# A mixture-of-experts kernel: the two fp32 x loads and the b1 load all issued by SyncE

## The chip, the core and the metric

The kernel runs on one core of one Trainium2 chip. The core has five engines that run side by side and wait for each other by semaphores: TensorE (PE in the profile, with its weight loads as PEld), VectorE (DVE), ScalarE (ACT), GpSimd (POOL) and SyncE (SP). Sixteen DMA engines move data between memory and the core; SP, ACT and POOL can issue transfers to them, each through a queue of its own (in the profile q1 for SP, q10 for ACT, q0 for POOL). The metric is the device time of one execution in microseconds (us), lower is better. The kernel before took 186.33 us, the median of four runs (185.84 to 186.41).

## The reference

Eight experts, each with its own two-layer network, its own 256 tokens of width 512, and 2048 hidden units. All inputs and the output are fp32.

```python
def reference(x, w1, w2, b1, b2):     # x (8,256,512)  w1 (8,512,2048)  w2 (8,2048,512)
    h = np.matmul(x, w1) + b1[:, np.newaxis, :]          # b1 (8,2048)
    h = np.maximum(h, 0)
    return (np.matmul(h, w2) + b2[:, np.newaxis, :]).astype(np.float32)   # b2 (8,512)
```

One expert's w1 and w2 are 4 MB each in fp32, so the weights are 64 MB in all, and each weight is used for 256 tokens.

## The kernel before, in words

**Two products per expert.** `first_product(e)` computes the hidden layer transposed. For each of 16 blocks of hidden units, four matmuls (L110) accumulate in PSUM a 128x256 block (128 hidden units, 256 tokens), and one ACT instruction (L117) adds b1, applies the ReLU and writes fp16. `second_product(e)` multiplies by w2: a small matmul puts b2 into the accumulator (L151), then 16 matmuls (L163) for each half of the tokens; DVE and ACT copy the two halves out (L130, L131), and a store goes out on SP (L137), for the last expert in four pieces on SP and ACT (L134, L135). The second product runs three experts behind the first (`LAG = 3`).

**Loads of weights.** w1 and w2 are loaded by POOL (L71, L82, and L90 for the last expert's w2 in six pieces), which converts them to fp16 on the way, so that 2 MB arrive for 4 MB read. They all use POOL's one queue. There are three buffers for w1 and three for w2. The list `loads` sets their order: per step x of an expert, w1 of that expert, then w2 of the expert three behind. Everything marked `ordered` keeps its program order on its engine. So the first three w1 loads are issued at once, and the fourth (for expert 3) waits on POOL until the first product of expert 0 has released its buffer.

**Loads of x.** Experts 2 to 7 get x through POOL's queue as fp16 (L65). The first two experts (`nXF32 = 2`) are loaded as fp32 into `x32`, outside of POOL's queue (L176), and DVE casts them (L189). x must stand transposed for the first product: eight TensorE transposes into PSUM (L97) and one DVE copy (L103) per expert.

**The stage in front, where the change is.** b1 is loaded as 16 rows of 1024 (`b1_rows`, L177), transposed by 64 small matmuls against an fp32 identity (L194), and copied by two DVE instructions to `b1T` (L202), the bias of every L117. On TensorE the program order is: the 64 matmuls of b1, the transposes of x of expert 0, the first product of expert 0. On DVE it is: cast of x of expert 0, cast of x of expert 1, the two copies to `b1T`, the copy of the transposed x. On ACT the program order before the first L117 is: load of x of expert 1 (L176), load of b1 (L177). On SP there is one load, x of expert 0, ahead of the first store, which it issues at 72 us.

Of the kernel before, what the change touches and what calls it, by code (L numbers as in the profile page):

```python
# [11 lines left out]
def kernel(  # L12
# [9 lines left out]
    nc = tc.nc  # L22
# [5 lines left out]
    nTB = T // P  # L28
# [25 lines left out]
    b1_rows = singles.tile([E * 2, M // 2], fp32)  # L54
# [14 lines left out]
    def load_w1(e):  # L69
        w1_sb[e] = w1_pool.tile([P, nKC, M], fp16, tag="w1", name="w1sb")  # L70
        ordered(nc.gpsimd.dma_start(  # L71
            out=w1_sb[e], in_=w1[e].rearrange("(p kc) m -> p kc m", kc=nKC)
        ))
# [99 lines left out]

    x32 = singles.tile([P, nXF32, nTB, H], fp32)
    for e in range(nXF32):
        (nc.sync if e == 0 else nc.scalar).dma_start(out=x32[:, e], max_dma_last_dim=2048, in_=x[e].rearrange("(p tb) h -> p tb h", tb=nTB))  # L176
    nc.scalar.dma_start(out=b1_rows, in_=b1.rearrange("e (s i) -> (e s) i", s=2))  # L177
    load_w1(0)
    ordered(nc.gpsimd.dma_start(  # L179
        out=b2_sb,  # L180
        in_=b2.rearrange("e h -> (e h)").rearrange("(o f) -> o f", o=1),
# [10 lines left out]
    for j in range(nJ):  # L192
        for s in range(2):
            ordered(nc.tensor.matmul(  # L194
                out=pb[s * 64 : (s + 1) * 64, j, :, :],
# [5 lines left out]
    for s in range(2):  # L201
        nc.vector.tensor_copy(  # L202
            out=b1T[s * 64 : (s + 1) * 64, :, :], in_=pb[s * 64 : (s + 1) * 64, :, :, s]
# [58 lines left out]
```

## Time and profile before

| | before |
|---|---|
| median of four runs | 186.33 us |
| the profiled execution's own time | 185.84 us |
| its span, first to last instruction | 183.9 us |
| PE busy, and mean granted clock | 139.8 us (76% of the span), 0.916 |
| ACT busy | 62.8 us (34%) |
| DVE busy | 13.4 us (7%) |
| DMA, all queues | 40.57 MB written, 221 GB/s over the span |
| share of the 16 DMA engines: q0 / q1 / q10 | 91.4% / 6.6% / 1.3% |

The profiled execution is the shortest of the four runs. Its span is 1.94 us shorter than its time: launch and end lie outside of it. The shares of the queues say how much of the sixteen DMA engines' time each one's packets took; their sum is close to 100%. Bytes are counted as written, so a weight load counts half of what it reads.

### The profile page before, as it was taken

The page shows a single profiled execution, that of the slowest core. Times are in us where ns is not written, and L with a number is a line of the kernel's source. Part 1 is how long each engine was busy: PE and PEld are TensorE (multiplying, and loading weights), DVE is VectorE, ACT ScalarE, POOL GpSimd, SP SyncE. Part 2 cuts the span into 40 slices and gives each one's busy share as a digit, 9 for nine tenths or more (in the row PEclk, how much of TensorE's full clock was granted, in tenths as well). Part 3 has the DMA queues.
Part 4 walks back from the last instruction along what each step waited for, and adds up shares of the span by engine and source line. Part 5 has one row for each costly group of instructions (what it writes and reads, how often), then busy time and mean ns, then how long its engine had stood idle before and what let it go on. Part 6 is the DMA issues. An engine that isn't in the chain of part 4 may idle for free.

```text
span 183.9 us, 2209 instructions
## 1 busy us (share of the span) xinstructions
PE 139.8 (76%) x946; PEld 99.6 (54%) x946; DVE 13.4 (7%) x22; ACT 62.8 (34%) x138; POOL 16.9 (9%) x37
## 2 busy tenths in 40 slices
PE   0546999399631999429994499946999994999991
PEld 0534889279521747328464374645649741344680
DVE  0320001001000110001100101001010010010101
ACT  0022689458540604505035060352408701010101
POOL 7100030300300002000110000100006100100000
PEclk9999999969995799956999659997899999699999
DMA  5998999899999999899999999999999999999993
GB/s 190 280 221 180 228 228 225 180 222 228 230 217 185 225 228 228 171 278 203 203 228 231 261 200 221 228 233 237 215 228 228 227 227 225 249 230 227 244 221 114
DMA packets 6488, 40.57 MB, mean 221 GB/s; under 512 B 688, under 2 KB 1728, under 8 KB 4432
## 3 DMA queue, kind: packets, MB, share of 16 engines
q0 software_dynamic: 4320, 35.14, 91.4%
q1 hardware_dynamic: 1568, 4.46, 6.6%
q10 hardware_dynamic: 592, 0.85, 1.3%
q8 instruction: 7, 0.11, 0.2%
q14 instruction: 1, 0.01, 0.0%
HBM read 71.39 MB, written 4.19 MB: 411 GB/s over the span
## 4 chain that ended last, share of the span: by engine, by line
DMA 58%; PE 34%; another core or an unknown queue 3%; POOL 2%; issue 1%; ACT 0%; ACTq 0%; POOLq 0%
DMA x<-in_x_dram 25%; DMA w2sb<-in_w_dram 21%; PE acc L163 20%; DMA w1sb<-in_w_dram 12%; PE ph L110 11%; PE psx L97 1%; PE acc L151 1%; POOL w1sb L71 1%; ACT out L131 0%; POOL b_sb L179 0%; POOL w2sb L82 0%; POOL ident masks.py:199 0%; ACTq L135 0%; POOL ident masks.py:197 0%
## 5 line engine op out<-in xcount | busy, mean ns | idle before, releaser
L110 PE MATMUL ph<-xT,w1sb 128*128 128x256 f16 x512 | 69.4, 303 | 8.8 <-DMA w1sb<-in_w_dram 8.8
L117 ACT ACTIVATE hT<-ph,b1T 128x256 f16<-128x256 f32 x128 | 57.0, 473 | 46.4 <-PE ph L110 46.3
L110 PEld LDWEIGHTS <-w1sb 128*128 128x128 f16 x512 | 62.1, 149 | 15.4 <-DMA w1sb<-in_w_dram 9.8
L163 PE MATMUL acc<-w2sb,hT 128*128 128x512 f16 x224 | 51.2, 388 | 2.3 <-DMA w2sb<-in_w_dram 2.3
L163 PEld LDWEIGHTS <-hT 128*128 128x128 f16 x288 | 28.0, 99 | 32.6 <-issue 7.9
L131 ACT COPY out<-acc 128x512 f32<-128x512 f32 (+1 forms) x9 | 4.9, 541 | 60.6 <-PE acc L163 60.6
L97 PE MATMUL psx<-ident,x 128*128 128x128 f16 x64 | 6.6, 265 | 22.7 <-DMA x<-in_x_dram 22.0
L97 PEld LDWEIGHTS <-x 128*128 128x128 f16 x64 | 5.3, 128 | 23.7 <-DMA x<-in_x_dram 22.9
L103 DVE COPY xT<-psx 128x1024 f16<-128x1024 f16 x8 | 5.5, 691 | 84.3 <-PE psx L97 84.3
L130 DVE COPY out<-acc 128x512 f32<-128x512 f32 (+1 forms) x9 | 5.7, 632 | 74.1 <-PE acc L163 74.1
L71 POOL DMA_DIRECT2D w1sb<-in_w_dram x8 | 4.4, 554 | 69.0 <-PE ph L110 68.2
L82 POOL DMA_DIRECT2D w2sb<-in_w_dram x8 | 4.3, 536 | 56.7 <-PE acc L163 56.7
L194 PE MATMUL pb<-ident,b_rows 16*64 16x16 f32 x64 | 3.7, 265 | 6.6 <-DMA b_rows<-in_b_dram 6.6
L163 PE MATMUL acc<-w,hT 128*128 128x256 f16 x64 | 7.4, 273 | 0.1
L194 PEld LDWEIGHTS pb<-ident,b_rows 16*64 16x64 f32 x64 | 3.6, 198 | 6.5 <-issue 6.5
L117 ACT ACT_TABLE_LOAD x1 | 1.3, 1283 | 11.0 <-DVE b1T L202 11.0
L151 PE MATMUL acc<-b_sb,ones 1*128 1x512 f16 (+1 forms) x18 | 4.8, 355 | 0.0
L90 POOL DMA_DIRECT2D w<-in_w_dram x6 | 3.6, 613 | 13.5 <-DMA w2sb<-in_w_dram 13.5
L65 POOL DMA_DIRECT2D x<-in_x_dram x6 | 3.3, 546 | 0.5 <-DMA w1sb<-in_w_dram 0.5
L151 PEld LDWEIGHTS <-ones 1*128 1x128 f16 x18 | 1.1, 92 | 2.1 <-issue 2.1
L189 DVE CAST x<-x 128x1024 f16<-128x1024 f32 x2 | 1.5, 734 | 4.3 <-DMA x<-in_x_dram 4.2
L202 DVE COPY b1T<-pb 64x128 f32<-64x128 f32 x2 | 0.6, 288 | 3.6 <-PE pb L194 3.6
(8 smaller groups left out, 2.0 us busy)
## 6 DMA issues: line engine op xcount, KB each, us to landing
w1sb<-in_w_dram POOLq DMA_DIRECT2D x8, 2048.0 KB, 33.6
w2sb<-in_w_dram POOLq DMA_DIRECT2D x6, 2048.0 KB, 47.6
out_dram<-out SPq DMA_DIRECT2D x7, 512.0 KB, 9.3
w2sb<-in_w_dram POOLq DMA_DIRECT2D x2, 1024.0 KB, 25.3
x<-in_x_dram POOLq DMA_DIRECT2D x6, 256.0 KB, 40.2
w<-in_w_dram POOLq DMA_DIRECT2D x3, 512.0 KB, 32.8
x<-in_x_dram ACTq DMA_DIRECT2D x1, 512.0 KB, 5.3
x<-in_x_dram SPq DMA_DIRECT2D x1, 512.0 KB, 4.4
```

The source lines that it names most:

```text
L71: ordered(nc.gpsimd.dma_start(out=w1_sb[e], in_=w1[e].rearrange("(p kc) m -> p kc m", kc=nKC)))
L82: ordered(nc.gpsimd.dma_start(out=t[:, lo : lo + step, :], in_=src[:, lo : lo + step, :]))
L90: ordered(nc.gpsimd.dma_start(out=t, in_=src[:, lo:hi, c0:c1]))
L97: ordered(nc.tensor.transpose(out=pt[:, kc, tb * P : (tb + 1) * P], in_=x16[e][:, tb, :].rearrange("p (q kc) -> p q kc", kc=nKC)[:, :, kc] ...
L103: nc.vector.tensor_copy(out=xT[e], in_=pt)
L110: ordered(nc.tensor.matmul(out=ph, lhsT=w1_sb[e][:, kc, :].rearrange("p (q j) -> p q j", j=nJ)[:, :, j], rhs=xT[e][:, kc, :], start=(kc == 0),
L117: nc.scalar.activation(out=hT[e][:, j, :], in_=ph, func=mybir.ActivationFunctionType.Relu, bias=b1T[:, j, e : e + 1], scale=1.0,)
L130: nc.vector.tensor_copy(out=out_sb[:, 0, :], in_=po[0])
L131: nc.scalar.copy(out=out_sb[:, 1, :], in_=po[1])
L151: ordered(nc.tensor.matmul(out=t, lhsT=ones1, rhs=b2_sb[0:1, e * H + c0 : e * H + c1], start=True, stop=False,))
L163: ordered(nc.tensor.matmul(out=acc[c0, tb], lhsT=hT[e][:, j, tb * P : (tb + 1) * P], rhs=t[:, j - lo, c0 - p0 : c1 - p0], start=False, sto ...
L194: ordered(nc.tensor.matmul(out=pb[s * 64 : (s + 1) * 64, j, :, :], lhsT=b1_rows.rearrange("r (q j) -> r q j", j=nJ)[:, :, j], rhs=ident[0 ...
```

## The change

The load of x of expert 1 and the load of b1 are issued by SP instead of ACT. All three loads of the front are then one after the other on SP: x of expert 0, x of expert 1, b1. Sizes, pieces and destinations stay as they are, and so do the instructions of TensorE, VectorE and GpSimd and their order. ACT's first instruction becomes the loading of its function table for L117, and ACT's first transfer is the store at L135 at the very end.

```diff
     for e in range(nXF32):
-        (nc.sync if e == 0 else nc.scalar).dma_start(out=x32[:, e], max_dma_last_dim=2048, in_=x[e].rearrange("(p tb) h -> p tb h", tb=nTB))
-    nc.scalar.dma_start(out=b1_rows, in_=b1.rearrange("e (s i) -> (e s) i", s=2))
+        nc.sync.dma_start(out=x32[:, e], max_dma_last_dim=2048, in_=x[e].rearrange("(p tb) h -> p tb h", tb=nTB))
+    nc.sync.dma_start(out=b1_rows, in_=b1.rearrange("e (s i) -> (e s) i", s=2))
     load_w1(0)
```

## The prediction

> **What bounds the kernel now.** I read the page's list of engines first: PE is busy for 76% of the span, no other compute engine for more than 34%. The queues add up to 99.5% of the sixteen DMA engines. So the first question is whether those engines ever rest. Busy time by stretches (columns: stretch in us, its length, PE, PEld, DVE, ACT and POOL busy, granted clock, DMA share, GB/s written):
>
> ```profile
> 1.00:2.00 1.00, 0.00 (x0) 0.00 (x0) 0.00 (x0) 0.00 (x0) 0.76 (x2) 1.00 0.23 20
> 2.00:3.00 1.00, 0.00 (x0) 0.00 (x0) 0.00 (x0) 0.00 (x0) 0.98 (x4) 1.00 0.78 231
> 3.00:4.00 1.00, 0.00 (x0) 0.00 (x0) 0.00 (x0) 0.00 (x0) 1.00 (x4) 1.00 1.00 377
> 4.00:5.00 1.00, 0.00 (x0) 0.00 (x0) 0.00 (x0) 0.00 (x0) 1.00 (x3) 1.00 1.08 416
> ...
> 100.00:140.00 40.00, 32.33 (x191) 21.60 (x192) 2.77 (x4) 12.24 (x28) 1.67 (x4) 0.87 1.04 230
> 140.00:178.00 38.00, 35.65 (x206) 20.29 (x205) 2.07 (x3) 7.81 (x17) 3.46 (x6) 0.96 1.02 235
> 178.00:180.00 2.00, 1.94 (x18) 1.45 (x15) 0.42 (x1) 0.37 (x1) 0.00 (x0) 1.00 0.39 55
> 180.00:184.00 4.00, 0.22 (x3) 0.00 (x0) 0.42 (x1) 0.37 (x1) 0.00 (x0) 1.00 0.40 131
> ```
>
> The second last column is what counts. From 3 us to 178 us the DMA engines are full; only the first microseconds and the last six are not. The bytes are the same after the change. So the end can move in three ways: the DMA engines begin earlier or later, they run dry somewhere because PE releases a weight buffer too late, or the tail changes.
>
> Next the front in order of time (start, duration, engine, line, what, and in brackets the idle time before and what ended it):
>
> ```profile
> 0.73 0.51 ACTq L176 DMA_DIRECT2D x<-in_x_dram  x1
> 0.74 0.42 SPq L176 DMA_DIRECT2D x<-in_x_dram  x1
> ...
> 1.26 0.49 ACTq L177 DMA_DIRECT2D b_rows<-in_b_dram  x1
> ...
> 5.18 1.55 DVE L189 CAST x<-x 128x1024 f16<-128x1024 f32 x2 [4.20 <-DMA x<-in_x_dram]
> ...
> 6.58 3.71 PE L194 MATMUL pb<-ident,b_rows 16*64 16x16 f32 x64 [6.58 <-DMA b_rows<-in_b_dram]
> 10.33 0.59 DVE L202 COPY b1T<-pb 64x128 f32<-64x128 f32 x2 [3.59 <-PE pb L194]
> ...
> 12.05 0.69 DVE L103 COPY xT<-psx 128x1024 f16<-128x1024 f16 x1 [1.13 <-PE psx L97]
> ...
> 15.55 6.66 PE L110 MATMUL ph<-xT,w1sb 128*128 128x256 f16 x36 [3.54 <-DMA w1sb<-in_w_dram]
> ```
>
> The reader is to see two clocks that meet at 15.55. The b1 chain starts when b1 lands (6.58) and ends with the transposed x at 12.05 + 0.69 = 12.74. The first weights land at about 15.5. So the b1 chain has 15.55 - 12.74 = 2.81 us to spare.
>
> Third, the rows of transfers (issues, size of one, median us from issue to landing), and for the first 7 us the packets of each queue:
>
> ```profile
> out_dram<-out SPq DMA_DIRECT2D x7, 512.0 KB, 9.3
> x<-in_x_dram ACTq DMA_DIRECT2D x1, 512.0 KB, 5.3
> x<-in_x_dram SPq DMA_DIRECT2D x1, 512.0 KB, 4.4
> ```
>
> ```profile
> q1 hardware_dynamic: 272, 0.52, 24.1%
> q10 hardware_dynamic: 304, 0.59, 23.0%
> ```
>
> **The change, part by part.** The built program shows that the change does what it says: ACT loses two DMA issues, SP has three in a row, PE's and POOL's order is the same, and DVE's two casts only wait on exchanged semaphores.
>
> *ACT without its two issues.* ACT saves 0.51 + 0.49 us between 0.73 and 1.75. Its next work, the table load, starts at 11.00, held by the `b1T` copy. Worth nothing.
>
> *SP with two more.* At 0.42 us an issue, x of expert 1 is issued at about 1.16 instead of 0.73, and b1 at about 1.58 instead of 1.26. SP's next instruction is a store at 72.13, so nothing is queued behind them. The cost can only come from the packets.
>
> *The packets.* q1 and q10 together bring 0.52 + 0.59 = 1.11 MB, and at the 416 GB/s of the stretch from 4 to 5 us this takes 2.67 us of all lanes, whichever queue they stand in. x of expert 0, alone for a time, lands sooner than its 4.4 us; x of expert 1 and b1 follow in the same queue. If one queue keeps the lanes as full as two, b1 lands when it did, about 6.5. Bounds: the stretch from 2 to 3 us is filled to 0.78, so closing its gap gains at most 0.22 us; if the second load opens a gap as long as its later issue, 0.42 us are lost. q10's stretches without q1 are not told apart in these rows, so I take the middle near zero, +0.1. For the end of the span this is -0.22 to +0.42, because the weights follow on the same lanes and stay full to 178 us.
>
> *b1's chain.* Later by 0.42, or by 0.85 at most (two whole issues), it ends at 13.2 to 13.6 instead of 12.74 and is hidden by the wait for the first weights at 15.55. It is the first cover. If it goes, there is a second: the fourth w1 load is issued only when PE is done with expert 0's first product, at 26.02 on POOL. At that time the third w1 load still occupies the DMA engines, and PE waits for it:
>
> ```profile
> 36.98 5.83 PE L110 MATMUL ph<-xT,w1sb 128*128 128x256 f16 x36 [3.26 <-DMA w1sb<-in_w_dram]
> ```
>
> So the fourth could be issued up to 36.98 - 26.02 = 10.96 us later before the lanes run dry. Only a b1 that lands later by more than 2.81 + 10.96 = 13.8 us, at about 20.3, moves the end. Before that PE is merely late for weights that are not there yet.
>
> *The casts on DVE.* The first may start earlier than 5.18, the second follows x of expert 1; both are done before b1's matmuls end at 10.29. Nothing.
>
> *The tail.* ACT's first transfer of the program is now the store at L135, on the path to the end:
>
> ```profile
> 179.84 0.99 SPq L134 DMA_DIRECT2D out_dram<-out  x2
> 180.00 0.37 ACTq L135 DMA_DIRECT2D out_dram<-out  x1
> ...
> 180.82 0.35 ACTq L135 DMA_DIRECT2D out_dram<-out  x1
> ```
>
> These stores land 2.1 us after issue, the last at 182.9, and the span ends at 183.9. The trace does not show what a first use of ACT's queue costs. The nearest row is the pair of x loads: issued at the same time, with the same size, ACT's landed after 5.3 us and SP's after 4.4. If all of the 0.9 us is first use and the second store queues behind the first, the end is 0.9 later; if only the first store is late it lands at 180.00 + 2.1 + 0.9 = 183.0, 0.1 later; if the 0.9 us is the sharing of lanes, it is 0. Nothing speaks for a gain. I take 0, since the issue at 180.82 has its own landing time and two loads that share 2.67 us of lanes cannot both be first.
>
> *Sum.* -0.22 to +0.42 in front, 0 to +0.9 in the tail: -0.2 to +1.3, likeliest +0.1. Against the profiled execution (span 183.9 and 1.94 around it, 185.84, the shortest of the four) that is 185.9; against the median 186.33 it is 186.4.
>
> **A rule against the row.** The seven output stores of 512 KB take 9.3 us where the load of the same size at the start took 4.4: a small transfer that meets the weight stream takes turns with it. The Trainium skill, "DMA: Bandwidth & Descriptors", section on queues, rings and completion order, says why: each DMA engine goes round the queues that have work, packet by packet. By this rule three loads in one queue get every second turn against the weights, where two queues got two turns of three; this speaks against the change, but only for what is left when the weights begin, and would give a later b1 inside the first cover, so +0. The same page's section on issuing engines says that issuing from several engines saves only issue time; by it the sum would be 0 as well, with 0.85 us as the price on SP. The rows of the front (1.00 and 1.08 full from 3 us on) agree with the second; no row of before shows what the first makes of these loads.
>
> **Rivals.**
> *The tail, slower.* ACT's first transfer is paid at the end instead of in front. For it: the 0.9 us between the x loads, and that the path ends with this store. Against: both loads wanted the same lanes. Price +0.9: 187.2. It decides from +0.56 us (0.3%) on, so from a first use that costs more than about 0.65 in both stores.
> *b1 caught behind the weights, slower.* If the weights reach the lanes before the single queue has been served, x of expert 1 and b1 take turns with large weight packets. A store of 512 KB took 9.3 us in that way, its longest 15.4. q10's count (304 packets for 0.59 MB) says that x comes in pieces of 2 KB, 256 of them; q1's stores have 4 KB rows, 128, so x would need twice as many turns: 18.6 to 30.8 us. Issued at 1.16, it would land at 20 to 32, b1 after it, against the 20.3 from which the lanes run dry: +0 to +12, so 186.4 to 198. For it: q10's load lands at 6.0, close to when the weights start. Against: from 3 to 5 us the lanes are full with 1.11 MB of x and b1, and the same bytes fit again. With a few pieces left behind, the two covers take it.
> *A front that is faster.* Closing the gap from 2 to 3 us gives -0.22: 186.1, inside 0.3%. No row gives more.
>
> **How the numbers follow.** 0.3% of 186.33 is 0.56 us, about what a measurement of this kernel can tell from no change (the four runs themselves spread over 0.57). Covers hold, within 0.3%: 0.58. Tail: 0.17, slower. b1 behind the weights by enough to matter: 0.08, slower. Causes that I can't name, such as the granted clock in PE's last 24 us, which runs at 0.93 to 1.00 without a wait: 0.13 faster, 0.04 slower. So faster 0.13, same 0.58, slower 0.29. The range holds the first case, the small gain and the tail: 185.7 to 187.3, which leaves out the 0.08 and about half of the unnamed.
>
> **What would show it.** Right: the first L110 still at 15.4 to 15.7, behind a wait for w1; b1's first matmul between 6.3 and 7.4; the first cast before 5.18; DMA share 1.0 from 3 to 178 us; the ACT stores landing after 2.0 to 2.2 us. Wrong in front: b1's first matmul after 9.4, then PE's first L110 moves; after 20, then the DMA share drops near 37 us. Wrong in the tail: L135's landing near 3.0.

## The result and the profile after

The changed kernel takes 186.33 us, the median of 48 executions (185.77 to 187.08, and one of 191.61), beside 186.10 us for 72 executions of the kernel before (185.69 to 186.62). A second slow execution, of 191.40 us, is on record outside of the 48, and the ratio leaves both out. The ratio is 1.0012 with a 95% interval of 1.0007 to 1.0018: about 0.22 us slower, inside the 0.3% that the forecast called no change. The profiled execution took 186.23 us with a span of 184.3 us.

The end hardly moved, but the front did. The front of the changed kernel in order of time (start, duration, engine, line, what, idle time before it and what ended it):

```profile
0.74 0.94 SPq L176 DMA_DIRECT2D x<-in_x_dram  x2
...
1.24 0.68 POOL L71 DMA_DIRECT2D w1sb<-in_w_dram  x1 [0.80 <-POOLq L246]
1.73 0.46 SPq L177 DMA_DIRECT2D b_rows<-in_b_dram  x1
...
4.12 0.78 DVE L189 CAST x<-x 128x1024 f16<-128x1024 f32 x1 [3.14 <-DMA x<-in_x_dram]
...
6.55 0.69 DVE L189 CAST x<-x 128x1024 f16<-128x1024 f32 x1 [1.65 <-DMA x<-in_x_dram]
...
9.21 3.73 PE L194 MATMUL pb<-ident,b_rows 16*64 16x16 f32 x64 [9.21 <-DMA b_rows<-in_b_dram]
...
14.70 0.69 DVE L103 COPY xT<-psx 128x1024 f16<-128x1024 f16 x1 [1.13 <-PE psx L97]
15.63 6.69 PE L110 MATMUL ph<-xT,w1sb 128*128 128x256 f16 x36 [0.97 <-DMA w1sb<-in_w_dram]
```

x of expert 0 comes 1.06 us sooner (4.12 for 5.18), b1 2.63 us later (9.21 for 6.58). The transposed x is ready at 14.70 + 0.69 = 15.39, only 0.24 us before the first L110 at 15.63, which still waits for w1. Of the first cover of 2.81 us (the time that b1's chain has to spare before the weights are there) nearly all is used.

Where did b1 wait? The packets that began between 5.2 and 7.6 us, by queue (packets, MB, share of the sixteen DMA engines), first in the kernel before:

```profile
q0 software_dynamic: 31, 0.51, 99.1%
q10 hardware_dynamic: 13, 0.00, 0.9%
```

and in the changed kernel:

```profile
q0 software_dynamic: 27, 0.44, 87.0%
q1 hardware_dynamic: 27, 0.07, 7.8%
```

Before, b1's data had passed by 5.2 us and only the small closing packets were left. After, all of b1's 64 KB (0.07 MB) stands in this stretch, in between weight packets of 16 KB (0.44 MB in 27).

The DMA engines and the tail are as they were. Busy time by stretches of the changed kernel (second last column: DMA share):

```profile
1.00:2.00 1.00, 0.00 (x0) 0.00 (x0) 0.00 (x0) 0.00 (x0) 0.76 (x2) 1.00 0.13 16
2.00:3.00 1.00, 0.00 (x0) 0.00 (x0) 0.00 (x0) 0.00 (x0) 0.98 (x4) 1.00 0.95 287
...
100.00:140.00 40.00, 31.83 (x188) 21.19 (x189) 2.77 (x4) 11.84 (x27) 1.28 (x3) 0.87 1.04 230
140.00:178.00 38.00, 35.66 (x206) 20.36 (x205) 2.07 (x3) 8.20 (x18) 3.85 (x7) 0.96 1.02 234
```

The gap between 2 and 3 us is closed (0.95 for 0.78), but the stretch before it is emptier (0.13 for 0.23), and the first weights are used 0.08 us later. ACT's two stores at the end land after 2.0 and 2.1 us, as before; the tail paid nothing for being ACT's first transfers.

### The profile page after: what moved, and what is told of

Its sections match the earlier page's. It is cut to its first block, busy times and chain, and to the rows that moved or that the text cites. A ratio compares the mean times of both kernels' runs of the same rounds, so it can differ in the third digit from the quotient of the medians.

```text
span 184.3 us, 2209 instructions
## 1 busy us (share of the span) xinstructions
PE 139.7 (76%) x946; PEld 99.7 (54%) x946; DVE 13.4 (7%) x22; ACT 62.8 (34%) x138; POOL 17.0 (9%) x37
## 4 chain that ended last, share of the span: by engine, by line
DMA 58%; PE 34%; another core or an unknown queue 3%; POOL 2%; issue 1%; ACT 0%; ACTq 0%; POOLq 0%
DMA x<-in_x_dram 25%; DMA w2sb<-in_w_dram 21%; PE acc L163 20%; DMA w1sb<-in_w_dram 12%; PE ph L110 11%; PE psx L97 1%; PE acc L151 1%; POOL w1sb L71 1%; ACT out L131 0%; POOL b_sb L179 0%; POOL w2sb L82 0%; POOL ident masks.py:199 0%; ACTq L135 0%; POOL ident masks.py:197 0%
## 5 line engine op out<-in xcount | busy, mean ns | idle before, releaser
L110 PE MATMUL ph<-xT,w1sb 128*128 128x256 f16 x512 | 69.3, 302 | 6.1 <-DMA w1sb<-in_w_dram 6.1
L117 ACT ACTIVATE hT<-ph,b1T 128x256 f16<-128x256 f32 x128 | 57.0, 473 | 44.1 <-PE ph L110 44.0
L110 PEld LDWEIGHTS <-w1sb 128*128 128x128 f16 x512 | 62.2, 149 | 12.5 <-DMA w1sb<-in_w_dram 7.0
```

The source lines that it names most:

```text
L110: ordered(nc.tensor.matmul(out=ph, lhsT=w1_sb[e][:, kc, :].rearrange("p (q j) -> p q j", j=nJ)[:, :, j], rhs=xT[e][:, kc, :], start=(kc == 0),
L117: nc.scalar.activation(out=hT[e][:, j, :], in_=ph, func=mybir.ActivationFunctionType.Relu, bias=b1T[:, j, e : e + 1], scale=1.0,)
```

## The experiments

All times are compared with the kernel before in the same series. The covers hold, by the profile above; what asks for a test is whether they are why the end stands still, what put b1 behind the weights, and what the remaining 0.12% is. For the last there were two theories at first: theory 1, that a late b1 sometimes eats through the cover; theory 2, that two loads of x in one queue cost it, whatever b1 does.

**One part at a time.** Two runs, each with one of the two moves, shown as edits to the changed kernel; the kernel before has x of expert 1 and b1 on ACT.

```diff
 # x1_alone: x of expert 1 on SP, b1 on ACT
-    nc.sync.dma_start(out=b1_rows, ...)
+    nc.scalar.dma_start(out=b1_rows, ...)
 # b1_alone: b1 on SP, x of expert 1 on ACT
-        nc.sync.dma_start(out=x32[:, e], ...)
+        (nc.sync if e == 0 else nc.scalar).dma_start(out=x32[:, e], ...)
```

> One part of the change alone: x of expert 1 moves to SP, b1 stays on ACT and is alone in its queue. Theory 1: b1 lands before 5 us, ratio 0.9995 to 1.0005. Theory 2: about 1.0012. It also shows whether the gap of the lanes between 2 and 3 us (0.78 full before, 0.95 after) belongs to two queues that start together: then a short gap again; if it belongs to the 256 pieces of x on ACT, no gap.

> The other part alone: b1 moves to SP behind x of expert 0, x of expert 1 stays on ACT. b1 is issued at about 1.2 us and follows 0.5 MB instead of 1.0 MB in its queue, so it should land before 6 us and before the weights reach the lanes. Theory 1: ratio 0.9995 to 1.0005. Theory 2: the same. A ratio of 1.0012 here would say that neither holds and that b1's queue itself costs.

Measured: 186.07 us, ratio 1.0000 (0.9991 to 1.0008), for x alone, and 186.18 us, 1.0001 (0.9993 to 1.0010), for b1 alone. Neither part costs anything that can be seen; the intervals leave room for up to 0.1%. With x alone b1's first matmul began at 4.13, with b1 alone at 6.45, no later than before (6.58). In the first of them the stretch from 2 to 3 us was filled to 0.69 and the cast of x of expert 1 began only at 10.89: there its last pieces were caught, and the cover took that too (first L110 15.77).

**b1 first.** All three loads on SP, b1 ahead.

```diff
+    nc.sync.dma_start(out=b1_rows, ...)
     for e in range(nXF32):
         nc.sync.dma_start(out=x32[:, e], ...)
-    nc.sync.dma_start(out=b1_rows, ...)
```

> All three loads on SP as in the change, but b1 ahead of the two x loads. Theory 1 (the change's 0.1% comes from b1 that lands late and eats the cover): b1's first matmul before 5 us instead of 9.21, and no difference to the kernel before, ratio 0.9995 to 1.0005. Theory 2 (it comes from two x loads in one queue, whatever b1 does): the ratio stays at about 1.0012. Either way the first L110 at 15.4 to 15.7 behind w1.

Measured: 189.20 us, ratio 1.0154 (1.0129 to 1.0180). Both theories expected no more than 0.12%. b1 was early, as expected, but now the third load in the row was x of expert 1, and the front shows what became of it:

```profile
0.74 0.38 SPq L175 DMA_DIRECT2D b_rows<-in_b_dram  x1
...
1.17 0.93 SPq L177 DMA_DIRECT2D x<-in_x_dram  x2
1.24 0.68 POOL L71 DMA_DIRECT2D w1sb<-in_w_dram  x1 [0.80 <-POOLq L246]
...
4.48 0.69 DVE L189 CAST x<-x 128x1024 f16<-128x1024 f32 x1 [3.50 <-DMA x<-in_x_dram]
...
23.95 0.69 DVE L189 CAST x<-x 128x1024 f16<-128x1024 f32 x1 [18.77 <-DMA x<-in_x_dram]
```

The second cast starts at 23.95: x of expert 1 has taken turns with the weights for 18 us. The packets that began between 5.2 and 24 us:

```profile
q0 software_dynamic: 279, 3.79, 94.8%
q1 hardware_dynamic: 264, 0.51, 7.9%
```

On PE, in the same kernel:

```profile
25.20 1.04 PE L97 MATMUL psx<-ident,x 128*128 128x128 f16 x8 [18.32 <-DVE b1T L202]
27.02 5.62 PE L110 MATMUL ph<-xT,w1sb 128*128 128x256 f16 x36 [0.78 <-DVE xT L103]
```

PE waits 18.32 us for `b1T`, whose copies stand behind that cast on DVE, and the first product begins at 27.02 instead of 15.55. This gave theory 3: what is issued before the first w1 load runs ahead of it, what is issued after it takes turns.

**w1 issued a little later.** POOL builds the identities first, in the changed kernel and in the one with b1 first. w1's issue moves from 1.24 to 1.62 (0.38 us, not the 0.9 us of the expectation).

```diff
+    make_identity(nc, ident)
+    make_identity(nc, ident16)
     load_w1(0)
     ordered(nc.gpsimd.dma_start(out=b2_sb, ...))
-    make_identity(nc, ident)
-    make_identity(nc, ident16)
```

> The changed kernel, but POOL builds the two identities before it issues the first w1 load, so that w1 is issued 0.9 us later, after SP has issued b1 (its issue ended at 2.19 us). Theory 3: what was issued before the first w1 load runs ahead of it on the DMA engines, what was issued after it takes turns with its packets; b1 is then ahead again. It expects b1's first matmul before 7 us instead of 9.21, and a ratio of 0.9995 to 1.0008. Theory 2 (one queue for both x costs the 0.1%, whatever b1 does): 1.0012. If the issue times don't decide, b1's matmul stays at about 9.

> b1 ahead of the two x loads on SP, as in the run that took 1.5% longer, and w1 issued 0.9 us later, after all three. Theory 3: x of expert 1 is no longer caught behind w1, its cast starts before 7 us instead of 23.95, first L110 near 16, ratio 0.999 to 1.002. If x of expert 1 is caught because b1 stands first, whatever w1 does: cast near 24 and ratio 1.015 again.

Measured, in the changed kernel: b1's first matmul at 7.24 for 9.21 (8.42 to 11.55 in the three further profiles below), first L110 at 16.38, ratio 1.0028 (1.0017 to 1.0038). With b1 first: the second cast at 6.06 for 23.95, first L110 at 15.88, ratio 1.0023 (1.0011 to 1.0035). 0.38 us of POOL's issue time is enough to free both loads. That is theory 3's expectation for the place of the loads, in both kernels, and it removes most of the 1.5%. Packets that began between 3.0 and 4.5 us with b1 first and w1 at its old place:

```profile
q0 software_dynamic: 16, 0.26, 89.2%
q1 hardware_dynamic: 183, 0.34, 59.5%
```

and with b1 first and w1 later:

```profile
q1 hardware_dynamic: 298, 0.58, 101.6%
```

In the first, sixteen weight packets have come in between; in the second the row is unbroken. But both later-w1 kernels are 0.2 to 0.3% slower than before although only closing packets are caught. A loss of this size needs no late b1; but here the weights themselves come later (first L110 16.38 and 15.88 for 15.55), a likely cause of its own, so these two runs do not say what the changed kernel's 0.12% is made of. What speaks against theory 1 is a run below: a b1 that passes the first cover by far (1.0007, at most 1.0018) costs no more than the change itself.

**The cast out of the way.** b1 first, w1 at its old place, and DVE's cast of x of expert 1 behind everything that expert 0 needs (the copies to `b1T` and of the transposed x, kept in this order).

```diff
-    for e in range(nXF32):
+    for e in range(1):
         x16[e] = ...; nc.vector.tensor_copy(out=x16[e], in_=x32[:, e])
 ...
     transposes(0)
+    for e in range(1, nXF32):
+        x16[e] = ...; ordered(nc.vector.tensor_copy(out=x16[e], in_=x32[:, e]))
```

> b1 ahead of the two x loads, w1 at its usual place, and on DVE the cast of x of expert 1 placed behind the b1T copies and the copy of the transposed x of expert 0. x of expert 1 lands at about 23 as before, but nothing of expert 0 waits for it. If the 1.5% came through DVE's order (the cast that waits in front of b1T), the first L110 is back at 15 to 16, PE waits 1 to 2 us at the transposes of expert 1 near 22, and the ratio is 0.999 to 1.003. If a late x costs on the DMA engines themselves, it stays near 1.015.

Measured: ratio 1.0021 (1.0012 to 1.0031), first L110 at 15.24. x of expert 1 is still late (its cast begins at 25.36), PE waits for it at the transposes of expert 1 for 5.29 us, more than the 1 to 2 us expected, and loses almost nothing at the end:

```profile
15.24 5.59 PE L110 MATMUL ph<-xT,w1sb 128*128 128x256 f16 x36 [6.55 <-DMA w1sb<-in_w_dram]
25.36 0.69 DVE L208 CAST x<-x 128x1024 f16<-128x1024 f32 x1 [15.95 <-DMA x<-in_x_dram]
26.12 1.04 PE L97 MATMUL psx<-ident,x 128*128 128x128 f16 x8 [5.29 <-DVE x L208]
```

So 1.3 of the 1.5% came through DVE's order. The rest, 0.39 us, is open: the stretch from 2 to 3 us is filled to 0.54 only, but with b1 alone it was filled to 0.65 and no loss could be seen.

**How much lateness the end forgives.** b1 moved to POOL's queue, behind the first w1 and behind the second.

```diff
 # b1_after_w1_0
-    nc.sync.dma_start(out=b1_rows, ...)
     load_w1(0)
     ordered(nc.gpsimd.dma_start(out=b2_sb, ...))
+    ordered(nc.gpsimd.dma_start(out=b1_rows, ...))
 # b1_after_w1_1: the same, with load_w1(1) ahead of the load of b1
```

> b1 is loaded by POOL's queue right behind the first w1 and b2, so that it lands at about 16 us, 9 us later than before and beyond the first cover of 2.81 us by 6 to 7 us. The prediction's second cover (the DMA engines stay full until about 37 us whatever PE does) expects the first L110 at about 22 us and an unchanged end: ratio within 0.998 to 1.003. Rival: PE's start sets the end, then +6.5 us, ratio 1.035. Theory 1, if the small loss grows with b1's lateness, expects more than 1.0012.

> b1 on POOL's queue behind the second w1, landing at about 26 us; first L110 at about 32.2, 16.6 later than before. The prediction's second cover ends when the lanes run dry: with 2.81 + 10.96 us of cover for b1 the loss is 16.6 - 10.96 = 5.7 us (ratio 1.031); if the lanes run dry earlier by the 2 us that the run with b1 first seems to show (L110 11.5 late, 2.9 us lost), 7.7 to 8.1 us (1.042). A ratio under 1.01 would say that the DMA engines do not set the end.

Measured: behind the first w1, first L110 at 22.41, 6.86 us later than before, ratio 1.0007 (0.9995 to 1.0018). Behind the second, first L110 at 32.24, 16.69 later, 193.64 us, ratio 1.0403 (1.0381 to 1.0424). The DMA share says why; from 35 to 40 and from 40 to 60 us, behind the first w1:

```profile
35.00:40.00 5.00, 5.00 (x52) 5.00 (x51) 0.69 (x1) 4.58 (x12) 0.71 (x2) 1.00 1.02 210
40.00:60.00 20.00, 11.75 (x109) 11.24 (x108) 0.77 (x2) 10.50 (x24) 2.48 (x5) 0.91 1.04 221
```

and behind the second:

```profile
35.00:40.00 5.00, 5.00 (x45) 4.70 (x44) 0.69 (x1) 3.94 (x9) 0.00 (x0) 1.00 0.30 56
40.00:60.00 20.00, 20.00 (x193) 20.00 (x192) 1.38 (x2) 19.16 (x45) 4.78 (x9) 1.00 0.86 176
```

1.02 and 1.04 are the values of the kernel before. With 0.30 and 0.86 the DMA engines lose 5 x 0.72 + 20 x 0.18 = 7.2 us, and 0.0403 x 186.04 = 7.5 us are lost in all. The fourth w1 was issued at 42.11 here; the engines had been empty from about 37.2, and its first packet began at about 43.3. PE late by 6.9 us costs nothing that can be measured, DMA engines that stand still cost their time.

**Three more profiles of the changed kernel, and x exchanged.** Theory 4 says that what is caught behind w1's first packets differs from execution to execution, and that a later b1 takes longer. The first three have no edit. In the last run x of expert 0 is on ACT, x of expert 1 and b1 on SP. Each is a single execution, beside one of 186.19 us of the kernel before.

```diff
 # swapped
-        nc.sync.dma_start(out=x32[:, e], ...)
+        (nc.scalar if e == 0 else nc.sync).dma_start(out=x32[:, e], ...)
```

> The changed kernel once more, for a second profile of it. Theory 4: the three loads end so close to the start of the weights that it differs from execution to execution what is caught behind w1's first packets; b1's first matmul then moves between the looks by steps of about 1.2 us (one large packet), from about 8 to 12, and a look with a later b1 takes longer. If b1's first matmul is at 9.2 within 0.3 us in all looks, the place of b1 is fixed and the wider spread of the changed kernel's times has another cause.

> As the look before: theory 4 expects b1's first matmul to differ between the looks by about 1.2 us or more; the other case, 9.2 within 0.3 us.

> As the two looks before: theory 4 expects b1's first matmul to differ between the looks by about 1.2 us or more; the other case, 9.2 within 0.3 us.

> x of expert 0 issued by ACT, x of expert 1 and b1 by SP. It tells what made ACT's x load 0.9 us slower than SP's in the kernel before. If ACT's first transfer costs more by itself, the load on ACT is again the slower one (5.3 us against 4.4), and the first cast starts at about 6 instead of 5.2. If it is the sharing of the lanes by two loads of 512 KB, the two differ by less than 0.3 us or the order turns round. The time within 0.3% either way.

Measured: b1's first matmul at 8.42, 9.09 and 11.55 us in the three profiles, with 186.54, 186.30 and 186.12 us. The front of the third:

```profile
8.85 0.69 DVE L189 CAST x<-x 128x1024 f16<-128x1024 f32 x1 [3.94 <-DMA x<-in_x_dram]
11.55 3.71 PE L194 MATMUL pb<-ident,b_rows 16*64 16x16 f32 x64 [11.55 <-DMA b_rows<-in_b_dram]
```

Theory 4's first half holds: what is caught differs from execution to execution; in the third even the last of x of expert 1 was, and the first L110 began at 17.78, behind the cover. Its second half isn't borne out: the execution with the latest b1 is the shortest of the three, but three that lie within 0.42 us can't settle it. With x exchanged (186.15 us) the load on ACT landed after 5.4 us and SP's after 4.6; the first cast began at 6.15, so ACT's load is again the slower one.

## Why the prediction was right or wrong

**The forecast of no change was right, and for its main reason.** The DMA engines are full from 3 to 178 us, and PE's lateness in front is forgiven as long as they stay so. The run with b1 behind the first w1 shows it alone: 6.86 us late on PE, 1.0007 (0.9995 to 1.0018). That the time itself, 186.33 us, lies so close to the forecast 186.4 is in part luck: the forecast started from 186.33 for the kernel before, which came out at 186.10, and the change cost 0.22 us where +0.1 was likeliest.

**b1's place was wrong.** The step that failed is the one on the packets: "If one queue keeps the lanes as full as two, b1 lands when it did, about 6.5", with 0.85 us later as its bound. From 2 us on the queue did keep the lanes full (0.95 and more), but b1 came 2.63 us later, and the sign of being right, a first matmul between 6.3 and 7.4, failed in all four profiles. The bytes in front of b1 were counted, not who else would be let in. In its issues SP took 0.47 us each instead of the 0.42 assumed, so b1 was issued from 1.73 to 2.19, after POOL had issued w1 (1.24 to 1.92); before, its issue had ended at 1.75. The rule of turns, packet by packet, which I had weighed and left at "a later b1 inside the first cover, so +0", was what b1 then met, and its price was as given there: inside the cover, by 0.24 us in the profile, and outside of it in one of three further profiles, at no cost to the end that can be seen.

**The front's gain of 0.22 us did not come.** The gap from 2 to 3 us closed from 0.78 to 0.95, but from 1 to 2 us the share fell from 0.23 to 0.13, so that 0.10 of the 0.17 us was lost again. Of the 0.07 us that are left nothing shows either: the first L110 was 0.08 us later, not earlier.

**The first cover (2.81 us) was sized right; the second (10.96 us) was too large.** The two runs that passed it give 11.47 us late for 0.0154 x 186.14 = 2.87 us lost, and 16.69 late for 7.50 lost. If every microsecond beyond the cover is lost in full, 8.6 to 9.2 us of PE's lateness are forgiven, and b1's first matmul could begin at about 18 us, not 20.3 (estimates from these two runs). The term took the time until PE needs the third w1, 36.98; but a load must be issued before the DMA engines run dry by the time that it takes to begin. With b1 behind the second w1 that was 1.2 us (42.11 to 43.3, with empty engines), which leaves about 9.8 of the 10.96, still a little more than the 8.6 to 9.2. With b1 first the fourth w1 was issued at 36.45, and the engines ran short; the kernel before, then the one with b1 first:

```profile
35.00:40.00 5.00, 3.02 (x18) 2.57 (x19) 0.00 (x0) 1.48 (x4) 0.62 (x2) 0.78 1.02 210
40.00:60.00 20.00, 11.58 (x102) 10.79 (x101) 0.72 (x2) 9.74 (x22) 1.60 (x3) 0.84 1.04 221
```

```profile
35.00:40.00 5.00, 5.00 (x49) 5.00 (x48) 0.00 (x0) 5.00 (x12) 1.59 (x3) 1.00 0.89 154
40.00:60.00 20.00, 14.97 (x145) 14.73 (x143) 1.38 (x2) 14.64 (x34) 3.19 (x6) 0.94 1.00 212
```

By these shares 5 x 0.13 + 20 x 0.04 = 1.45 of its 2.87 us were lost there. Another 0.39 us may be what the run with the late cast lost too; the rest is open.

**The tail was right at 0.** ACT's stores land after 2.0 to 2.1 us, although they are its first transfers. The 0.9 us between the two x loads isn't the cost of a first use wherever it falls: it stayed with ACT when x was exchanged (5.4 against 4.6), but only at the start of the program. The sharing of the lanes alone, from which the prediction argued, doesn't explain it either, so the 0 was right in part for a reason that wasn't.

**The rival with b1 caught behind the weights** had the right mechanism and, for the changed kernel, too large a price: one or two turns of a 64 KB load, where 16 turns of 512 KB were priced. With b1 first those were met: x landed at about 23.9, inside the 20 to 32 us of the rival, at a loss of 1.5%.

**What stays open** is the 0.12%. Neither part alone has it (1.0000 and 1.0001, each to within 0.1%), and a much later b1 does not raise it beyond the noise (1.0007, at most 1.0018); the two kernels in which b1 is early again have a loss of their own. In the profiled pair it arises neither in front nor in the tail: on the chain that ended last the changed kernel is 0.03 us behind at 35 us (35.09 for 35.06), 0.37 behind where the next x load has landed (82.06 for 81.69) and 0.40 at the last store. In between both kernels issue the same loads, so one pair of executions may show no more than the spread of their times. That spread is wider in the changed kernel, and I have no profile of the two executions at 191.40 and 191.61 us, some 5 us longer, where none of the 72 of before is above 186.62. Their granted clock, 0.937, is no lower than in the others (0.913 to 0.935) and as in the kernels with PE very late (0.932 to 0.938); that more of x of expert 1 was caught in them, as with b1 first, would fit, but is not shown.

## What to carry to other kernels

Where the DMA engines are full all through, ask of an edit in front whether it starts the stream earlier or later and whether it lets it run dry; whether an engine is late by some microseconds is the second question. When a small load moves behind others in a queue, compare the end of its issue with the issue of the big stream: here 0.4 us of issue order decided whether 512 KB landed at 6 or at 24 us. It is no guarantee: twice the last pieces of a load that had been issued in time were caught. And look for what stands behind the late load on an engine that works in order: one cast on DVE in front of `b1T` turned a late x of expert 1, which nobody needed yet, into 1.3% of the kernel.

## What was not expected of the hardware

- A transfer issued before the first weight load mostly ran through without weight packets in between. In the run with b1 first, weight packets began before 4.5 us with w1 issued at 1.24; in the changed kernel, with the same issue time, the packets between 3.0 and 4.5 us are x alone, up to 3.3 us after w1's issue began, where 1.2 us were enough with empty engines:

```profile
q1 hardware_dynamic: 312, 0.61, 104.3%
```

- The Trainium skill, "DMA: Bandwidth & Descriptors", section on queues, rings and completion order, has each DMA engine go round the queues packet by packet. The runs agree with it only from the moment at which the weights had got in; of the 512 KB loads issued ahead of w1, those of before, of the changed kernel (but for the third of its further profiles) and of the two kernels with w1 later passed whole or nearly so. The kernel with x alone on SP and that third profile don't fit the simple order of issues: x of expert 1 was issued by 1.68 and 1.69, and its last pieces were caught (cast at 10.89 and 8.85).
- At the start of the program a load on ACT's queue was slower than one of the same size on SP's, both issued at 0.73 to 0.74: x 5.3, 5.3 and 5.4 us against 4.4, 4.6 and 4.6 in the kernel before, with b1 alone and with x exchanged. b1 at the head of its queue, in two different runs, took 3.3 us on ACT and 2.1 us on SP. At the end both queues' stores take 2.0 to 2.1 us.
